# Decays counted from the middle of each two-chunk block, and a memory pool of their own for the joins, in a hybrid encoder layer

## The chip, the cores and the metric

The kernel runs on one core of one Trainium2 chip. The metric is the device time of one execution in microseconds (us). The engines are TensorE (PE, with its weight loads as PEld), VectorE (DVE), ScalarE (ACT), GpSimd (POOL) and SyncE (SP, which here only issues transfers). Each engine works through its own instructions in the order in which they stand in the program; an instruction that waits holds up everything behind it on its engine. SP and POOL issue loads and stores in their order too, and ACT issues some.

## The reference, cut to what matters

One layer: a SwiGLU feed-forward network, a mixer, and a second feed-forward network, on 1024 tokens of width 1024 in float32. The mixer projects its input once, computes attention on eight heads and a two-directional delta-rule scan (RWKV-7) on eight other heads, and projects both to the output. The change lies in the scan, whose step for one direction and head is

```python
def _rwkv7_step(state, inp):
    r, w, k, v, kk, kka = inp
    sa = jnp.einsum('dbhvk,dbhk->dbhv', state, kk)
    state = state * w[..., None, :] - sa[..., :, None] * kka[..., None, :] + v[..., :, None] * k[..., None, :]
    y = jnp.einsum('dbhvk,dbhk->dbhv', state, r)
    return state, y
...
    w_logit = w0 + jnp.einsum('bsdr,drc->bsdc', jnp.tanh(wd), w2)
    decay = jnp.exp(-jnp.exp(-jax.nn.softplus(-w_logit) - 0.5))
...
    h = h + 0.5 * _rmsnorm(f, ffn1_post_g[l])
    z = _rmsnorm(h, mix_pre_g[l]) @ w_in[l]
    y_att = _attention_group(z[..., :ATT_IN], cos, sin, attn_out_g[l])
    y_rwkv = _rwkv7_group(z[..., ATT_IN:], ...)
    mix = jnp.concatenate([y_att, y_rwkv], axis=-1) @ w_out[l]
    h = h + _rmsnorm(mix, mix_post_g[l])
```

The state is 64x64 per head and direction. Each step multiplies it by a decay, so that over several steps the product of decays, the exponential of a running sum of their logarithms, is what counts.

## The kernel before, in words

The sequence is cut into 16 chunks of 64 steps (C), and two chunks make one of 8 blocks (BLK = 2, TB = 128 steps). Both directions go side by side (d = 0 and 1), and eight heads are held as four pairs (pr) on the two halves of the partitions (par).

`low_rank` (lines 547 to 577) computes the logarithms of the decays for all steps, sums them up within each chunk with a scan along the row (line 576; `reset` starts the sum anew at each chunk) and stores the sums in HBM (`d_w`).

`prep` (lines 818 to 876) makes a block's operands, one direction after the other; a direction's part is called a prep half below. It loads the sums `cum` (the tile is named `th_w`) and the streams of keys, rates and receptances (`ka`, `kd`, `in`, the last from `d_rk`), and forms exp(cum) in `e` (line 840) and exp(-cum) in place (line 841). The column of `e` at a chunk's end, the decay over the whole chunk, is copied into `gc` (line 843), one column for each chunk. DVE multiplies kk and r by exp(cum) into `pr` (lines 845 and 846) and the keys and rates by exp(-cum) into `bk` (lines 849 and 851), ACT copies a piece of `bk` (line 850). PE then makes the scores `lp` (line 858), DVE masks them into `lm` (line 860), PE transposes `bk` into `bp` (line 866) and ACT copies that to `bt` (line 868). A piece of `lm` goes to HBM (`d_x`) and comes back as `X` in another layout.

`solve` (lines 878 to 898) inverts 64 triangular blocks of 32x32 on DVE in 31 pairs of short instructions on `ttmp` and `Ti` (lines 894 and 896) and a transpose (line 898).

`merge`, called the join below (lines 900 to 924), puts two inverses of 32 together to one of 64. Its matmuls are `pa` of lines 911, 916 and 922, its copies on ACT are `tt` of lines 912, 918 and 924 and `am` of line 919. The tile `am` lies in the pool `sc`, which the value streams' memory is given to once these are done.

`chain` (lines 938 to 994) is the sequential part. For each chunk PE computes `xu` from the chunk's scores and the state `sv` (line 963), ACT copies it to `xs` (line 966), PE multiplies by the joined inverse (`xu` again, line 974), ACT makes `uv` (line 976), and PE collects the new state in `st` and the outputs in `y` (both through the helper of line 959: `y<-pr,sv`, `st<-uv,bt`, `y<-lm,uv`). The old state is carried into `st` by a product with the identity (`st<-sv,ident`, all chunks but the first). DVE then makes the next state

```python
            if nx is not None:
                for par in range(2):
                    hs = half(par)
                    V.tensor_tensor(nx[hs, :, par], st[hs], gc[hs, :, :, i:i + 1].to_broadcast([64, 2, 4, 64]), op=OP.mult)
```

which is called the hand-over to the next chunk. The values come from HBM through loads of `uv` and `sv` that POOL issues (line 930).

Beside the chain lies other work: the prep halves of later blocks, their solves and joins, the attention half of the output projection (`project_attended`: `yat`, `yq`, `yah`, `yal`, `wol` and the matmuls `po`), and at the end the first finishing units (`yc`, `var`, `bonus`, `rstd`, `gate`) and the rest of the output projection (`pw`). Their order on each engine is set by a planner that gives each instruction a priority by its place in the code and a modelled cost, and puts it where it is expected to be ready; pools of memory hold a step back until their former users are done. No table written by hand sets it. The stages in time: the first feed-forward network to about 700 us, low-rank and value projections to 795, attention and the streams of the scan to 1180, the first preps from 1182, the joins and the chain from 1246 to 1549, finishing units and output projection to 1662, the second feed-forward network to the end.

## Time and profile before

| | us |
|---|---|
| median of 3 runs (2298.36 to 2302.42) | 2300.16 |
| the profiled execution's own time | 2300.81 |
| its span | 2299.0 |
| PE, DVE, ACT, POOL busy over the span | 2198.8, 1767.3, 1023.6, 537.0 |
| joins and chain, 1246.0 to 1548.5 | 302.5 |
| of this: before chunk 1's state is handed over (1292.8) | 46.8 |

Read the stage table by windows: for each stretch it gives an engine's busy time and number of instructions, the TensorE clock that was granted as a share of the full one, and the share of the transfer engines. The windows are cut where the second `sv` instruction of a hand-over to an even chunk ends. In a timeline row the first number is the start in us from the span's start and the second the time from the first start to the last end of the group; what stands in brackets is the idle time ahead of it and what ended it. PE's groups overlap by some tenths of a us, since matmuls are pipelined.

### The profile page before, as it was taken

The page shows a single profiled execution, that of the slowest core. Times are in us where ns is not written, and L with a number is a line of the kernel's source. Part 1 is how long each engine was busy: PE and PEld are TensorE (multiplying, and loading weights), DVE is VectorE, ACT ScalarE, POOL GpSimd, SP SyncE. Part 2 cuts the span into 40 slices and gives each one's busy share as a digit, 9 for nine tenths or more (in the row PEclk, how much of TensorE's full clock was granted, in tenths as well). Part 3 has the DMA queues.
Part 4 walks back from the last instruction along what each step waited for, and adds up shares of the span by engine and source line. Part 5 has one row for each costly group of instructions (what it writes and reads, how often), then busy time and mean ns, then how long its engine had stood idle before and what let it go on. Part 6 is the DMA issues. An engine that isn't in the chain of part 4 may idle for free. (4 is left out here: it accounts for less than half of the span.)

```text
span 2299.0 us, 41391 instructions
## 1 busy us (share of the span) xinstructions
PE 2198.8 (96%) x15556; PEld 1781.8 (77%) x15556; DVE 1767.3 (77%) x2893; ACT 1023.6 (45%) x1925; POOL 537.0 (23%) x673
## 2 busy tenths in 40 slices
PE   7999999999999998999998899999799999999998
PEld 5788888878877676777776777776678888888887
DVE  7999999865676254677679678747999999997566
ACT  5322323354567411666654644455442323335453
POOL 2354443410000011222221111122024444441000
PEclk9999999999999999999999799999899999999999
DMA  5354545486662513654467746357445454548665
GB/s 151 124 183 151 170 147 173 164 266 193 193 225 78 212 72 105 186 147 144 131 178 184 211 136 167 107 173 257 155 135 174 150 174 151 170 152 282 194 194 187
DMA packets 346700, 387.74 MB, mean 169 GB/s; under 512 B 73474, under 2 KB 249346, under 8 KB 346500
## 3 DMA queue, kind: packets, MB, share of 16 engines
q1 hardware_dynamic: 294928, 271.71, 39.2%
q0 software_dynamic: 31216, 100.73, 11.6%
q10 hardware_dynamic: 20356, 12.66, 1.8%
q8 instruction: 122, 2.00, 0.4%
q14 instruction: 78, 0.64, 0.1%
HBM read 258.06 MB, written 126.94 MB: 167 GB/s over the span
## 5 line engine op out<-in xcount | busy, mean ns | idle before, releaser
L81 PE MATMUL gu<-xh,wh 128*128 128x512 f32 x704 | 277.3, 394 | 4.6 <-ACT wh L186 4.5
L186 ACT ACTIVATE wh<-raw 128x512 fp32r<-128x512 f32 (+1 forms) x273 | 168.3, 627 | 252.3 <-PE gu L81 95.7
L81 PE MATMUL gu<-xl,wh 128*128 128x512 f32 x704 | 276.0, 392 | 0.0
L81 PE MATMUL gu<-xh,wl 128*128 128x512 f32 x704 | 275.9, 392 | 0.0
L187 DVE TENSOR_TENSOR wl<-raw,wh 128x512 fp32r<-128x512 f32 (+1 forms) x273 | 270.4, 994 | 3.7 <-ACT wh L186 3.0
L421 PE MATMUL pd<-gl,gwh 128*128 128x512 f32 x616 | 240.6, 391 | 2.6 <-DVE gl L187 2.6
L421 PE MATMUL pd<-gh,gwh 128*128 128x512 f32 x616 | 239.8, 390 | 0.6 <-DVE row L86 0.6
L421 PE MATMUL pd<-gh,gwl 128*128 128x512 f32 x616 | 240.1, 390 | 0.2 <-DVE gwl L187 0.2
L86 DVE TENSOR_TENSOR row<-gu,row 128x512 f32<-128x512 f32 x308 | 206.6, 683 | 25.8 <-PE gu L81 23.5
L187 DVE TENSOR_TENSOR gwl<-graw,gwh 128x512 fp32r<-128x512 f32 (+2 forms) x187 | 118.8, 643 | 124.0 <-ACT gwh L186 122.3
L116 POOL DMA_DIRECT2D d_hid<-row x154 | 84.7, 551 | 546.0 <-DVE row L114 524.2
L186 ACT ACTIVATE gwh<-graw 128x512 fp32r<-128x512 f32 (+2 forms) x187 | 103.1, 554 | 187.2 <-PE pd L421 151.3
L81 PEld LDWEIGHTS gu<-xh,wh 128*128 128x128 f32 x704 | 133.4, 190 | 33.6 <-ACT wh L186 5.6
L81 PEld LDWEIGHTS gu<-xh,wl 128*128 128x128 f32 x704 | 133.2, 189 | 27.7 <-DVE wl L187 0.2
L81 PEld LDWEIGHTS gu<-xl,wh 128*128 128x128 f32 x704 | 133.3, 189 | 27.4
L421 PEld LDWEIGHTS pd<-gl,gwh 128*128 128x128 f32 x616 | 115.7, 188 | 27.8 <-DVE gl L187 3.9
L421 PEld LDWEIGHTS pd<-gh,gwh 128*128 128x128 f32 x616 | 115.6, 188 | 25.5 <-DVE row L86 1.0
L421 PEld LDWEIGHTS pd<-gh,gwl 128*128 128x128 f32 x616 | 115.7, 188 | 24.1 <-DVE gwl L187 0.6
L187 DVE TENSOR_TENSOR gl<-raw,gh 128x512 fp32r<-128x512 f32 x160 | 114.7, 728 | 22.9 <-ACT gh L186 22.6
L94 ACT ACTIVATE row<-row 128x512 f32<-128x512 f32 x44 | 27.8, 633 | 212.0 <-DVE row L86 212.0
L145 POOL TENSOR_TENSOR ws<-ws 128x512 f32<-128x512 f32 x88 | 114.6, 1303 | 1.2
L186 ACT ACTIVATE gh<-raw 128x512 fp32r<-128x512 f32 x160 | 98.1, 622 | 35.5 <-DMA raw<-in_ffn_w_down_dram 22.8
(364 smaller groups left out, 5238.2 us busy)
## 6 DMA issues: line engine op xcount, KB each, us to landing
d_hid<-row POOLq DMA_DIRECT2D x154, 256.0 KB, 2.5
graw<-d_hid SPq DMA_DIRECT2D x132, 256.0 KB, 2.9
raw<-in_ffn_w_gate_dram SPq DMA_DIRECT2D x88, 256.0 KB, 3.1
raw<-in_ffn_w_up_dram SPq DMA_DIRECT2D x88, 256.0 KB, 3.6
ws<-in_ffn_w_down_dram SPq DMA_DIRECT2D x88, 256.0 KB, 4.1
d_ws<-ws POOLq DMA_DIRECT2D x88, 256.0 KB, 2.3
raw<-d_ws SPq DMA_DIRECT2D x88, 256.0 KB, 2.8
raw<-in_ffn_w_down_dram SPq DMA_DIRECT2D x66, 256.0 KB, 3.6
```

Source lines behind the costliest of these rows:

```text
L81: self.K.nc.tensor.matmul(ps, a[:, k, :], b[:, k, :], start=(k == 0 and i == 0), stop=(k == 3 and i == 2))
L86: add = lambda o, x: V.tensor_tensor(o, ps, x, op=OP.add)
L94: A.activation(y[:, 0], y[:, 0], AF.Silu)
L116: put = lambda n, y: G.dma_start(self.hid[n - 1, j // 2], y)
L145: G.tensor_tensor(o, a, b, op=OP.subtract)
L186: self.nc.scalar.activation(h, src, AF.Copy)
L187: (eng or self.nc.vector).tensor_tensor(l, src, h, op=OP.subtract)
L421: T.matmul(ps[x], a[:, ts], b, start=(m == 0 and k == 0), stop=(m == NM - 1 and k == 2))
```

## The change

Two things are changed. First, the sums of the first chunk of each block are shifted by the sum at that chunk's end (`mid`, kept in an unused piece of the tile `edge`), so that within a block all exponentials count from its middle. The state at the hand-over from an even to an odd chunk then needs no decay: `st` holds only the new products, and DVE adds the old state (`st` + `sv`). At the odd chunk's end the old state is still brought in by the identity product, and the decay of the second chunk and that of the next block's first are applied together: `gc` is the exponential of `cum`'s last column plus the next block's `mid`. Second, the join's tile `am` moves to a pool `joins` of its own, beside the two block pools.

In numbers: PE loses the four `st<-sv,ident` instructions of the seven even chunks after the first (28, which the trace records as 56). DVE gains eight copies of 128x8 and eight subtractions of 128x512 in `low_rank`; 16 `gc` copies become 14 additions of 128x4; the 30 state instructions are 2 copies, 14 products and 14 additions. ACT gains 16 exponentials of 128x4 and 7 of 128x8 (`gc`). POOL loses one memset. The transfers are the same in number. Since `gc` now reads `cum`, the exponential in place that follows it on ACT (line 846 of the changed kernel) comes after it.

```diff
@@ -574,6 +574,9 @@
                     V.tensor_tensor_scan(o, reset, o, 0.0, op0=OP.mult, op1=OP.add)
+                    first, mid = o.rearrange("p (n i t) -> p n i t", i=BLK, t=C)[:, :, 0], self.mid[:, d, pr]
+                    V.tensor_copy(mid, first[:, :, C - 1])
+                    V.tensor_tensor(first, first, mid[:, :, None].to_broadcast([128, NC_ // BLK, C]), op=OP.subtract)
                 self.nc.sync.dma_start(self.lr_d[nm][d][pr], o)
@@ -822,7 +825,7 @@
         lm = big.tile([128, 2, 2, BLK, 4, 128], F32, name="lm", tag="lm")
-        gc = big.tile([128, 2, 4, BLK], F32, name="gc", tag="gc")
+        gc = big.tile([128, 2, 4, BLK], F32, name="gc", tag="gc")[:, :, :, 0]
         blk = dict(lm=lm, pr=[], bt=[], gc=gc)
@@ -836,14 +839,15 @@
             e1 = self.e1
-            e4 = e1.rearrange("p (a i) t -> p a i t", i=BLK)
-            A.activation(e4[:, :, :, 1:C + 1], chunks(cum), AF.Exp)
+            if n + 1 < NC_ // BLK:
+                V.tensor_tensor(gc[:, d], cum[:, :, TB - 1], self.mid[:, d, :, n + 1], op=OP.add)
+            A.activation(e1[:, :, 0], self.mid[:, d, :, n], AF.Exp, scale=-1.0)
+            A.activation(e1[:, :, 1:], cum, AF.Exp)
             A.activation(flat(cum), flat(cum), AF.Exp, scale=-1.0)
             ei = chunks(cum)
-            V.tensor_copy(gc[:, d], e4[:, :, :, C])
             pt = big.tile([128, 4, BLK, 128], F32, name="pr", tag=f"pr{d}")
-            V.tensor_tensor(pt[:, :, :, 0:C], chunks(x["kk"]), e4[:, :, :, 0:C], op=OP.mult)
-            V.tensor_tensor(pt[:, :, :, C:], chunks(x["r"]), e4[:, :, :, 1:C + 1], op=OP.mult)
+            V.tensor_tensor(pt[:, :, :, 0:C], chunks(x["kk"]), chunks(e1[:, :, 0:TB]), op=OP.mult)
+            V.tensor_tensor(pt[:, :, :, C:], chunks(x["r"]), chunks(e1[:, :, 1:]), op=OP.mult)
             bk = p.tile([128, 4, BLK, 192], F32, name="bk", tag="bk", bufs=2)
@@ -868,6 +872,8 @@
                 blk[k].append(v)
+        if n + 1 < NC_ // BLK:
+            A.activation(gc, gc, AF.Exp)
         for par in range(2):
@@ -902,7 +908,7 @@
         NI, lm = 2 * BLK * 4, blk["lm"]
-        D, am = blk["inv"], p.tile([128, NI, 32], F32, name="am", tag="d11")
+        D, am = blk["inv"], p.tile([128, NI, 32], F32, name="am", tag="am")
         blk["tt"] = tt = self.tt[n % 2]
@@ -964,7 +970,7 @@
             A.copy(xs, xu)
-            if not first:
+            if i:
                 for d in range(2):
@@ -980,14 +986,19 @@
                 add(st[half(par), d, pr, :], bt[d][:, i, par, pr, :], uv[:, d, par, pr, :],
-                    first and d == 0 and pr == 0, True)
+                    not i and d == 0 and pr == 0, True)
             for d, pr, par in heads:
...
                     hs = half(par)
-                    V.tensor_tensor(nx[hs, :, par], st[hs], gc[hs, :, :, i:i + 1].to_broadcast([64, 2, 4, 64]), op=OP.mult)
+                    if i:
+                        V.tensor_tensor(nx[hs, :, par], st[hs], gc[hs, :, :, None].to_broadcast([64, 2, 4, 64]), op=OP.mult)
+                    elif first:
+                        V.tensor_copy(nx[hs, :, par], st[hs])
+                    else:
+                        V.tensor_tensor(nx[hs, :, par], st[hs], sv[hs, :, par], op=OP.add)
             for d in range(2):
@@ -1174,8 +1185,7 @@
         G, io = self.nc.gpsimd, self.io
-        self.e1 = p.tile([128, 4 * BLK, C + 1], F32, name="e1")
-        G.memset(self.e1[:, :, 0:1], 1.0)
+        self.e1 = p.tile([128, 4 * (TB + 2)], F32, name="e1").rearrange("p (a t) -> p a t", a=4)[:, :, :TB + 1]
         self.unit = p.tile([128, 2, 16], F32, name="unit")
@@ -1196,6 +1206,7 @@
             self.edge = self.pool(top, "edge", side="right").tile([128, 120], F32, name="edge")
+            self.mid = self.edge[:, 24:88].rearrange("p (d a n) -> p d a n", d=2, a=4)
             self.constants()
@@ -1271,7 +1282,7 @@
                 self.project_values(ring, psum, x, vw, range(5, NT))
-            s_mc, s_at, s_sc, s_ps = (ExitStack() for _ in range(4))
+            s_mc, s_at, s_sc, s_ps, s_mi = (ExitStack() for _ in range(5))
             self.mix_constants(self.pool(s_mc, "mixc", **R))
@@ -1290,6 +1301,7 @@
             R0, R1 = (self.pool(s_sr, f"blk{j}", 1, **R) for j in range(2))
+            mi = self.pool(s_mi, "joins", 1, **R)
             self.scan_constants(sp)
@@ -1317,18 +1329,19 @@
             rs_a = self.rstd(eo, self.ss_a.rearrange("p a b -> p (a b)"), NT * H, 1.0 / HD, EPS)
-            self.merge(0, blk[0], sc, pm)
+            self.merge(0, blk[0], mi, pm)
             upto(2)
...
                 if n + 1 < NB:
-                    self.merge(n + 1, blk[n + 1], sc, pm)
+                    self.merge(n + 1, blk[n + 1], mi, pm)
                 if n == NB - 1:
...
                     self.project_attended(eo, sc, pe, t, WA, rs_a)
+            s_mi.close()
             s_sr.close()
```

The order of the instructions moves with it, from the last projection of the streams to the end of the chain. Line numbers are those of the changed kernel in the rows of after. The counts here are instructions; the trace records two for each `lp`, `xu`, `pa`, `y` and `st`, and one for each `po`, `bp` and `yq`.

PE after the last matmul of the streams (`zr`), before: the first join's last two products (916, 922) stand behind the transposes of the values (`vt`) and among the scores of the third block.

```order
L523 MATMUL zr<-xh_5416,zl 128x512
L911 MATMUL pa<-ident,X 32x32 x64
L640 MATMUL vt<-ident,us 128x128 x8
L640 MATMUL vt<-ident,vrev 128x128 x4
L858 MATMUL lp<-pr,bk 128x128 x5
L640 MATMUL vt<-ident,vrev 128x128 x4
L858 MATMUL lp<-pr,bk 128x128 x11
L866 MATMUL bp<-ident,bk 128x64 x16
L916 MATMUL pa<-X,lm 32x32 x32
L858 MATMUL lp<-pr,bk 128x128 x6
L922 MATMUL pa<-tt_12073,am 32x32 x32
L858 MATMUL lp<-pr,bk 128x128 x10
```

And after: line 917 is the old 911, 922 the old 916, 928 the old 922.

```order
L523 MATMUL zr<-xh_5416,zl 128x512
L917 MATMUL pa<-ident,X 32x32 x64
L922 MATMUL pa<-X,lm 32x32 x32
L643 MATMUL vt<-ident,us 128x128 x8
L928 MATMUL pa<-tt_12097,am 32x32 x26
L643 MATMUL vt<-ident,vrev 128x128 x4
L928 MATMUL pa<-tt_12097,am 32x32 x6
L862 MATMUL lp<-pr,bk 128x128 x6
L643 MATMUL vt<-ident,vrev 128x128 x4
L862 MATMUL lp<-pr,bk 128x128 x10
L870 MATMUL bp<-ident,bk 128x64 x16
L862 MATMUL lp<-pr,bk 128x128 x16
```

The first join now stands ahead of most of the value transposes, and its copies on ACT likewise stand ahead of them; the join of the second block (the old 911) stands behind the chain's first `xu` where it stood ahead of it. On SP the load of `in` for the second half of the third block's prep stands ahead of the last four `d_vt` stores and no longer behind them.

DVE at the hand-over from chunk 7 to chunk 8, before: the `pr` products of the next prep half stand ahead of the hand-over, its scores are masked (860) right behind it.

```order
L990 TENSOR_TENSOR sv<-st,gc 64x2x256
L896 TENSOR_TENSOR Ti<-Ti,ttmp 128x21x6
L990 TENSOR_TENSOR sv<-st,gc 64x2x256
L894 TENSOR_TENSOR ttmp<-X,Ti 128x120
L843 COPY gc<-e_11074 128x8
L896 TENSOR_TENSOR Ti<-Ti,ttmp 128x20x6
L894 TENSOR_TENSOR ttmp<-X,Ti 128x133
L896 TENSOR_TENSOR Ti<-Ti,ttmp 128x19x7
L894 TENSOR_TENSOR ttmp<-X,Ti 128x126
L860 TENSOR_TENSOR lm<-lp,k_tri 128x512
L896 TENSOR_TENSOR Ti<-Ti,ttmp 128x18x7
L860 TENSOR_TENSOR lm<-lp,k_tri 128x512
```

And after: `gc` of both directions follows the hand-over (997 is the old 990), and the `pr` and `bk` products of the prep (849, 853, 855) come behind that.

```order
L997 TENSOR_TENSOR sv<-st,gc 64x2x256
L900 TENSOR_TENSOR ttmp<-X,Ti 128x96
L997 TENSOR_TENSOR sv<-st,gc 64x2x256
L902 TENSOR_TENSOR Ti<-Ti,ttmp 128x24x4
L843 TENSOR_TENSOR gc<-th_w,edge 128x4 x2
L900 TENSOR_TENSOR ttmp<-X,Ti 128x115
L1099 TENSOR_TENSOR yat<-yat,rs 128x512
L902 TENSOR_TENSOR Ti<-Ti,ttmp 128x23x5
L849 TENSOR_TENSOR pr<-in_14722,e_11093 128x8x64
L900 TENSOR_TENSOR ttmp<-X,Ti 128x110
L853 SCALAR_TENSOR_TENSOR bk<-ka,th_w 128x8x64
L902 TENSOR_TENSOR Ti<-Ti,ttmp 128x22x5
```

PE at the same place, before: the first prep half's scores stand between chunk 7's last product and chunk 8's `xu`, the second half's behind chunk 8's `xu`.

```order
L959 MATMUL y<-lm,uv 64x64 x16
L858 MATMUL lp<-pr,bk 128x128 x16
L866 MATMUL bp<-ident,bk 128x64 x8
L1091 MATMUL yq<-ident,yat 128x128 x2
L866 MATMUL bp<-ident,bk 128x64 x8
L1091 MATMUL yq<-ident,yat 128x128 x2
L963 MATMUL xu<-sv,lm 64x64 x16
L959 MATMUL st<-sv,ident 64x256 x4
L974 MATMUL xu<-xs,tt_12073 64x64 x16
L959 MATMUL y<-pr,sv 64x64 x3
L858 MATMUL lp<-pr,bk 128x128 x12
```

And after: chunk 8's `xu` comes first, and the scores of both halves follow it, ahead of the product with the joined inverse (980).

```order
L969 MATMUL xu<-sv,lm 64x64 x16
L965 MATMUL y<-pr,sv 64x64
L1091 MATMUL po<-woh,yah 128x512
L1091 MATMUL po<-wol,yah 128x512
L1091 MATMUL po<-woh,yal 128x512
L862 MATMUL lp<-pr,bk 128x128 x16
L870 MATMUL bp<-ident,bk 128x64 x8
L1091 MATMUL po<-woh,yah 128x512
L870 MATMUL bp<-ident,bk 128x64 x8
```

The second half's scores and transposes follow with eight more `po`, and then the product of line 980. The last prep, of block 7, stands whole at the end of chunk 9, ahead of chunk 10's `xu`. The `po` instructions are spread anew: counted from each chunk's first `xu`, over chunks 0 and 1, 2 and 3, 4 and 5, 6 and 7, 8 and 9, 10 and 11, and from 12 on, they are 12, 36, 36, 12, 24, 60, 12 before and 0, 48, 36, 24, 24, 48, 12 after. One finishing unit (`yc` to `gate`) more stands within the chain's last four chunks. From the end of the chain on, the order is the same, but for eight loads of `row` that SP issues earlier.

## The prediction

> **What bounds the kernel now.** I read the page first, then the stage table of the chain, the waits there, and the timelines of PE, DVE, ACT and SP at the two places that the order rows show. The page says that PE is the engine to watch:
>
> ```profile
> span 2299.0 us, 41391 instructions
> PE 2198.8 (96%) x15556; PEld 1781.8 (77%) x15556; DVE 1767.3 (77%) x2893; ACT 1023.6 (45%) x1925; POOL 537.0 (23%) x673
> ```
>
> The change leaves all but low-rank, the joins and the chain as they were, so the stage table decides. A row has the window and its length, then the busy time of PE, PEld, DVE, ACT and POOL, then the granted clock of PE, the share of the transfer engines and GB/s; the first two rows are the stage before chunk 0 and chunks 0 and 1, then come blocks 1 to 5 and chunk 12.
>
> ```profile
> 1246.00:1279.60 33.60, 23.38 (x497) 20.34 (x496) 24.48 (x65) 19.20 (x31) 8.04 (x14) 0.61 0.97 246
> 1279.60:1303.20 23.60, 21.59 (x455) 18.84 (x449) 14.02 (x31) 16.17 (x30) 3.69 (x7) 0.76 0.61 167
> 1303.20:1344.30 41.10, 39.69 (x744) 32.47 (x743) 34.23 (x106) 19.55 (x36) 5.81 (x12) 0.96 0.54 155
> 1344.30:1383.00 38.70, 35.70 (x724) 30.59 (x722) 27.82 (x82) 18.94 (x34) 5.82 (x12) 0.91 0.55 156
> 1383.00:1417.10 34.10, 31.84 (x712) 26.70 (x711) 27.79 (x85) 17.61 (x32) 5.32 (x12) 1.00 0.59 168
> 1417.10:1454.80 37.70, 35.05 (x718) 29.17 (x718) 29.56 (x88) 18.23 (x33) 5.53 (x12) 0.91 0.52 139
> 1454.80:1501.30 46.50, 42.51 (x745) 34.82 (x744) 34.67 (x107) 18.99 (x35) 5.21 (x9) 0.93 0.35 98
> 1501.30:1524.30 23.00, 20.21 (x448) 16.95 (x447) 6.83 (x23) 9.22 (x17) 8.00 (x11) 0.78 0.88 293
> ```
>
> In blocks 1 to 5 PE is busy for 91 to 97% and DVE for 72 to 83%: PE's work, its clock and its short waits make the time there. The part of a block lost to the clock, its length times what is missing to 1.00, is 1.6, 3.5, 0, 3.4 and 3.3 us, 11.8 in all. Ahead of chunk 0 PE stands for 10.2 of 33.6 us and runs at 0.61. Among the waits of the stage, 1246 to 1550, PE's own is that for the masked scores (in us, times, longest):
>
> ```profile
> PE lp L858 <- DVE lm L860: 4.5, 5, 1.1
> ```
>
> **The start of the chain.** The rows of several engines here, in order of time:
>
> ```profile
> 1246.12 1.29 PE L911 MATMUL pa<-ident,X 32*32 32x32 f32 x128
> 1251.12 1.09 PE L640 MATMUL vt<-ident,us 128*128 128x128 f32 x4 [3.72 <-DVE us L538]
> 1257.92 2.71 SPq L644 DMA_DIRECT2D d_vt<-vts  x4
> 1260.68 0.52 SPq L182 DMA_DIRECT2D in<-d_rk  x1
> 1265.56 0.57 ACT L912 COPY tt<-pa 128x512 f32<-128x512 f32 x1
> 1266.18 1.92 PE L916 MATMUL pa<-X,lm 32*32 32x32 f32 x64 [2.72 <-ACT tt L912]
> 1267.34 0.69 DVE L845 TENSOR_TENSOR pr<-in,e 128x512 f32<-128x512 f32 x1 [1.87 <-DMA in<-d_rk]
> 1270.92 1.92 PE L922 MATMUL pa<-tt,am 32*32 32x32 f32 x64
> 1277.76 1.93 PE L911 MATMUL pa<-ident,X 32*32 32x32 f32 x128
> 1279.61 1.18 PE L963 MATMUL xu<-sv,lm 64*64 64x64 f32 x19
> ```
>
> The first join is ready for its copy at 1247.4 (its `pa` of line 911 has run) and gets it 18 us later. In the new order the copy and the two products stand ahead of most value transposes, where PE stood for 3.72 us, so 1.92 + 1.92 = 3.84 us leave the path to the first `xu`. The load of `in` goes out ahead of four `d_vt` stores that take 2.71 us to issue, and that takes the wait of 1.87 out. Line 911 of the second join (1.93) moves from ahead of `xu` to behind it, where PE has other work to wait beside; I count nothing for it. The clock is the rest: the same 128 instructions take 1.29 us at 1246.12 and 1.93 at 1277.76, and with 3.72 us less of standing I take some of it back, 2.3 us. Together -8.0. What was late there, the prep of block 2, stays late, and DVE work that stood ahead of chunk 0 (two `wol`, `yat`, `yal`, two `bk`, about 6 x 0.69 = 4.2 us) comes later, into block 1, where DVE has 41.10 - 34.23 = 6.9 us free; I charge +1.0 of it. From -10 (the waits' whole 3.84 + 1.87 and a faster clock for the 13 us up to `xu`) to 0 (DVE, or the loads of the values that POOL issues behind the `d_vt` stores, hold the first `xu` back). The four stores go out 0.5 us later behind the load.
>
> **The identity products.** One chunk's four, in the chain of waits:
>
> ```profile
> 1542.54 1.01 PE st L959 x8
> ```
>
> Seven chunks lose it: 7 x 1.01 = 7.1. It stands where PE waits for ACT's copy `xs`, so not all is won: in the five even chunks 2 to 10 the scores and `po` now fill that gap, in 12 and 14 only `y` products do, which moves but removes nothing. I take -5.0, with 0 and -7.1 as ends. At the hand-overs the addition of `sv` costs DVE what the product did.
>
> **The prep behind the hand-over.** In the old order a prep half was ready before the hand-over and its scores filled PE right behind it. Rows at the hand-over to chunk 8 (1417.05):
>
> ```profile
> 1417.28 0.16 DVE L843 COPY gc<-e 128x8 f32<-128x8 f32 x1
> 1418.48 0.63 ACT L841 ACTIVATE th_w<-th_w 128x512 f32<-128x512 f32 x1
> 1419.45 1.04 PE L858 MATMUL lp<-pr,bk 64*128 64x128 f32 x7 [1.14 <-DVE lm L860]
> 1423.62 0.68 DVE L849 SCALAR_TENSOR_TENSOR bk<-ka,th_w 128x512 f32<-128x512 f32 x1
> 1427.28 0.62 ACT L850 COPY bk<-bk 64x512 f32<-64x512 f32 x1
> 1430.77 0.39 PE L1080 MATMUL po<-wol,yah 128*128 128x512 f32 x1
> 1431.00 0.40 PE L1080 MATMUL po<-woh,yal 128*128 128x512 f32 x1
> ...
> 1407.79 1.15 PE L963 MATMUL xu<-sv,lm 128*64 128x64 f32 x31
> ...
> L896 DVE TENSOR_TENSOR Ti<-Ti,ttmp 128x126 f32<-128x126 f32 (+22 forms) x206 | 52.4, 254 | 5.4
> ```
>
> In the new one, two `gc` (2 x 0.16), the exponential in place (0.63), `bk` (0.68) with `yat` (taken like `bk`), `pr` (0.69 as in line 845's row) and some solve steps between, and the copy of `bk` (0.62) follow the hand-over one after the other: 0.3 + 0.6 + 2.1 + 0.6, with three solve steps of 0.25 some 4.4 us. PE has for it the new chunk's `xu` (1.15 at full clock, as in block 3) and, of the 15 `po` around it, about eleven still to do at 0.23 from start to start (1430.77 to 1431.00), 3.7 together. So a wait of 0.7 us opens where one of 0.9 on average (4.5 in 5) closes, but two halves now follow each other, and DVE must bring 8 `lm`, 2 `pr` and 4 `bk` operations there, 14 x 0.68 = 9.5 us beside its solve steps, for about as much of PE's scores, transposes and `po`. I charge 0.8 us for each of five boundaries, +4.0; the ends are -4.5 (the waits of `lp` go and none comes) and +18 (first rival).
>
> **Moved `po`.** Block 5, the longest, gives away 12 of 60 instructions, 12 x 0.23 = 2.8 us; chunks 6 and 7, where PE had 34.10 - 31.84 = 2.3 us idle, take 12. Half is won: -1.4, between 0 and -2.8. The 12 that leave chunk 1 go to chunks 2 and 3; even.
>
> **The tail.** One finishing unit more lies among the chain's last chunks. A unit's own time on PE, from the chain of waits:
>
> ```profile
> 1548.48 1.06 PE yc L1014 x2
> 1551.60 0.79 PE var L1018 x8
> 1552.38 0.97 PE bonus L1025 x2
> 1554.30 0.88 PE gate L1039 x4
> ```
>
> That is 3.7 us from after 1548.5 to before it, where PE stood for 2.8 us of 23.0 at 1501.30. The steps behind the chain have waits of their own, so I take -2.5, between 0 and -3.7.
>
> **What I cost at nothing.** The 16 new operations in `low_rank`, 8 x (0.16 + 0.69) = 6.8 us of DVE, lie ahead of a stretch in which DVE has none to do (first row below; the second row, of 1500 to 1600, prices ACT's small operations):
>
> ```profile
> 756.50:794.60 38.10, 36.45 (x133) 24.00 (x131) 0.00 (x0) 14.54 (x22) 2.70 (x5) 1.00 0.45 173
> L1020 ACT ACTIVATE edge<-var,gneps 128x8 f32<-128x8 f32 x8 | 2.1, 268 | 5.7 <-PE var L1018 5.7
> ```
>
> PE does not wait for them there; without that cover they would cost their 6.8. ACT's 23 small exponentials cost 0.27 each, 6.2 us, on an engine that is busy for about half of each block; only where they stand in the line to `lp` do they count, and there they come ahead of it. Uncovered, +6.2. POOL's memset and DVE's `gc` copies go and come even.
>
> **The sum.** -8.0 + 1.0 - 5.0 + 4.0 - 1.4 - 2.5 = -11.9 against the profiled 2300.81, which is 1.81 over its span and 0.65 over the median: 2288.9 us.
>
> **Short waits and the clock.** At 1419.45 PE waited 1.14 us, and from 1421 to 1427 its clock stood at 0.50; at 1406.34 it waited 1.05 and block 3 stayed at 1.00:
>
> ```profile
> 1421.00:1427.00 6.00, 6.00 (x55) 4.34 (x55) 5.11 (x15) 3.26 (x6) 0.00 (x0) 0.50 0.43 115
> 1406.34 0.82 PE L916 MATMUL pa<-X,lm 32*32 32x32 f32 x39 [1.05 <-issue]
> ```
>
> So a wait of some 1.1 us goes with a half clock in one place and not in the other; 6 us at 0.50 cost 3 us. [...]
>
> **The rivals.** Slower: the chain gc, exponential, `bk`, copy opens waits of more than about 1 us ahead of `lp`, for both halves of each prep, and each is followed by 6 us at half clock. Two in each of five blocks cost 10 x 3 = 30 us where the blocks now lose 11.8, so +18 in place of +4: 2288.9 + 14 = 2303. It decides from a wait of about 1 us on, and 0.7 is my estimate; for it speaks the row at 1419.45, against it the one at 1406.34.
>
> No change: DVE sets the blocks. It is busy for 27.8 to 34.7 us in them and takes 4.2 us more over from before chunk 0; if the joins' gain only moves its work, -8 + 1 becomes -2 and the identity's -5 becomes -2: 2300.81 - 2 - 2 + 4 - 1.4 - 2.5 = 2297. For it speaks that DVE's solve of a block (31 x 2 steps of 0.25, 15.7 us) must be done before the next join; against it that PE, not DVE, is busy for 91 to 97%.
>
> The change does not do what it says: the first join stays late, because its tile `tt` is cleared by POOL at 1252 and later or its copies wait elsewhere. Then the -8 + 1 falls to -1 and the time is 2295. For it speaks POOL's row before, with the memset behind the last `d_v` store; against it that the memset now stands ahead of that store:
>
> ```profile
> 1252.02 1.86 POOL L1188 MEMSET tt<- 128x1024 f32 x2
> ```
>
> More gain: with `xu` ahead of the scores PE's short waits vanish, and the 11.8 us of clock come back: 2277.
>
> **How the numbers follow.** Forecast 0.45, around 2289 by 5 to either side; more gain 0.18; no change 0.12; late join 0.08; slower 0.17. About 0.2%, 4.6 us, is what a measurement can tell from no change here. Faster: 0.43 + 0.18 + 0.05 + 0.04 = 0.70; slower: 0.17, same the remaining 0.13. The range reaches from 2273, somewhat below the greater gain, to 2305, just above the slower rival, and leaves out what lies beyond two of these mishaps together.
>
> **What would show it.** The first `xu` of chunk 0 some 8 us earlier, near 1272, and the hand-over to chunk 1 near 1285 and not at 1292.8; no `st<-sv,ident` at the even chunks; waits of `lp` on `bk` or on ACT below 1 us; blocks 1 to 5 together about 197 us (198.1 before), the chain's end near 1539, and from there to the end 2.5 us less. Wrong would be a granted clock below 0.9 in most blocks, waits of PE above 1 us ahead of `lp`, or a first `xu` still at 1279.

## The result, and the profile after

The changed kernel takes 2311.43 us (median of five runs, 2309.86 to 2313.99) where the kernel before takes 2300.16. The ratio is 1.0053, 95% interval 1.0033 to 1.0072; one of the five executions of the kernel before, of 5375.53 us, is left out of it. The changed kernel is slower by half a per cent; 2289 and a range up to 2305 had been forecast. The profiled execution took 2309.86 us, so it stands for the runs. Its page, first and third line:

```profile
span 2308.1 us, 41327 instructions
...
PE 2201.0 (95%) x15500; PEld 1784.7 (77%) x15500; DVE 1772.0 (77%) x2907; ACT 1023.8 (44%) x1948; POOL 538.7 (23%) x672
```

PE has 56 instructions less and still 2 us more busy time. The stage table is cut as the one of before: the stage ahead of chunk 0, chunks 0 and 1, blocks 1 to 5, and then in one row the time from the hand-over to chunk 12 to the chain's end (columns: window and length, busy PE, PEld, DVE, ACT, POOL, granted clock, DMA share, GB/s).

```profile
1245.40:1270.50 25.10, 18.89 (x354) 16.55 (x353) 20.69 (x59) 17.01 (x30) 7.18 (x11) 0.66 0.88 238
1270.50:1299.60 29.10, 21.69 (x577) 19.55 (x576) 13.72 (x32) 17.11 (x31) 5.40 (x11) 0.77 0.66 178
1299.60:1342.70 43.10, 40.42 (x734) 33.40 (x734) 36.06 (x107) 21.08 (x40) 5.01 (x11) 0.96 0.52 153
1342.70:1388.30 45.60, 39.22 (x711) 32.84 (x710) 27.56 (x80) 19.23 (x37) 5.62 (x12) 0.81 0.48 136
1388.30:1427.60 39.30, 35.28 (x711) 29.89 (x710) 27.20 (x82) 18.50 (x36) 5.94 (x12) 0.91 0.52 147
1427.60:1470.80 43.20, 36.05 (x641) 30.77 (x639) 31.50 (x89) 17.49 (x33) 5.97 (x11) 0.77 0.57 154
1470.80:1515.20 44.40, 42.27 (x808) 35.02 (x807) 38.05 (x123) 19.88 (x37) 5.24 (x9) 0.96 0.30 85
1515.20:1563.70 48.50, 44.85 (x966) 36.27 (x964) 17.14 (x32) 26.37 (x50) 16.43 (x22) 0.89 0.84 287
```

Blocks 1 to 5 take 43.1 + 45.6 + 39.3 + 43.2 + 44.4 = 215.6 us where they took 198.1: 17.5 more. That is more than the 9.1 us by which the spans differ. The rest went the right way: the hand-over to chunk 2 comes at 1299.6 (1303.2 before), and from the chain's end to the end of the span pass 744.3 us (750.6). Blocks 2 to 4 carry the loss, and blocks 2 and 4 have a clock of 0.81 and 0.77 (both 0.91 before). Among PE's waits in joins and chain, 1245 to 1564 (in us, times, longest), these five lead:

```profile
PE pa L917 <- issue: 8.2, 2, 4.4
PE lp L862 <- DVE bk L855: 6.4, 3, 3.9
PE pa L922 <- issue: 6.0, 4, 2.3
PE pa L928 <- issue: 2.6, 2, 1.6
PE lp L862 <- DVE ttmp L900: 2.6, 1, 2.6
```

Two kinds of wait have grown: that of the scores `lp` for the prep's `bk` (0.4 us before), and a wait put down to "issue", in which PE waits for nothing that the profile knows (16.8 us in these rows, 6.4 before; in blocks 1 to 5 alone 9.7 and 4.5). The row for `ttmp` lies ahead of block 1.

**The prep at a hand-over.** Rows of DVE, ACT and PE at the hand-over to chunk 4, in order of time:

```profile
1341.98 0.69 DVE L997 TENSOR_TENSOR sv<-st,gc 64x512 f32<-64x512 f32 x1
1342.91 0.24 DVE L843 TENSOR_TENSOR gc<-th_w,edge 128x4 f32<-128x4 f32 x2
1343.39 1.15 ACT L846 ACTIVATE th_w<-th_w 128x512 f32<-128x512 f32 x2 [0.76 <-DVE Ti L902]
1346.52 0.69 DVE L849 TENSOR_TENSOR pr<-in,e 128x512 f32<-128x512 f32 x1 [1.85 <-DMA in<-d_rk]
1347.33 0.68 DVE L853 SCALAR_TENSOR_TENSOR bk<-ka,th_w 128x512 f32<-128x512 f32 x1
1348.05 0.62 ACT L854 COPY bk<-bk 64x512 f32<-64x512 f32 x1 [2.92 <-DVE bk L853]
1348.88 3.78 PE L862 MATMUL lp<-pr,bk 64*128 64x128 f32 x24 [3.93 <-DVE bk L855]
```

And the 6 us from the start of these scores, and the next 6, as windows (the clock is the third number from the end):

```profile
1348.90:1354.90 6.00, 6.00 (x30) 5.03 (x31) 4.93 (x13) 1.83 (x4) 0.00 (x0) 0.50 0.85 248
1354.90:1360.90 6.00, 6.00 (x33) 4.39 (x33) 3.40 (x10) 1.17 (x2) 0.00 (x0) 0.50 0.35 100
```

`gc` starts within 0.3 us of the end of the hand-over, and `pr`, `bk`, the copy and `lp` follow one after the other. `gc` lies in the memory of the block, which goes round among three blocks, so it can't be written before the hand-over three blocks back has read its own. It now also reads `cum`, and so the exponential in place, and everything behind that, waits with it. PE stands for 3.93 us and then runs for 12 us at half clock. At the hand-over to chunk 8, which ends at 1427.56, the wait is 2.23 us and the clock 0.50 for the next 6 us; two operations of DVE wait there for their loads:

```profile
1429.25 0.69 DVE L1099 TENSOR_TENSOR yat<-yat,rs 128x512 f32<-128x512 f32 x1 [1.06 <-DMA yat<-d_ya]
1431.64 0.69 DVE L849 TENSOR_TENSOR pr<-in,e 128x512 f32<-128x512 f32 x1 [1.51 <-DMA in<-d_rk]
1433.96 4.28 PE L862 MATMUL lp<-pr,bk 64*128 64x128 f32 x29 [2.23 <-DVE bk L855]
```

Not all of the clock lost in the blocks follows the prep. In block 4 PE also stood in a join, for an issue wait, and ran the next 6 us at half clock:

```profile
1463.71 0.54 PE L917 MATMUL pa<-ident,X 32*32 32x32 f32 x21 [3.78 <-issue]
1463.80:1470.00 6.20, 6.20 (x151) 5.84 (x152) 2.36 (x7) 3.66 (x7) 1.19 (x2) 0.50 0.19 51
```

**Chunk 0.** PE from the first `xu` on, and DVE's state for chunk 1:

```profile
1270.45 0.32 PE L969 MATMUL xu<-sv,lm 64*64 64x64 f32 x2
1273.74 1.17 PE L917 MATMUL pa<-ident,X 32*32 32x32 f32 x114
1279.29 0.43 PE L917 MATMUL pa<-ident,X 32*32 32x32 f32 x14 [4.37 <-issue]
1284.78 1.92 PE L928 MATMUL pa<-tt,am 32*32 32x32 f32 x64 [1.12 <-ACT am L925]
...
1288.64 1.41 DVE L999 COPY sv<-st 64x512 f32<-64x512 f32 x2 [13.13 <-PE st L965]
```

The first `xu` stands 9.2 us earlier than before (1279.61), and the hand-over ends at 1290.1, only 2.7 earlier (1292.8): the second join lies between the two, with a standing of 4.37 us within the instructions of one line.

### The profile page after: what moved, and what is told of

It reads as the page before. It is cut to its first block, busy times and chain, and to the rows that moved or that the text cites. A ratio compares the mean times of both kernels' runs of the same rounds, so it can differ in the third digit from the quotient of the medians.

```text
span 2308.1 us, 41327 instructions
## 1 busy us (share of the span) xinstructions
PE 2201.0 (95%) x15500; PEld 1784.7 (77%) x15500; DVE 1772.0 (77%) x2907; ACT 1023.8 (44%) x1948; POOL 538.7 (23%) x672
## 4 chain that ended last, share of the span: by engine, by line
PE 40%; DVE 5%; DMA 3%; issue 2%; ACT 2%; SPq 0%; POOL 0%; DVEq 0%; ACTq 0%; POOLq 0%
PE gu L81 18%; PE pd L421 9%; PE zr L523 1%; PE po L1091 1%; PE lp L862 1%; PE pw L1091 1%; PE st L965 1%; DVE Ti L902 1%; DVE ttmp L900 1%; DMA in<-d_rk 1%; PE y L965 1%; PE xu L980 1%; PE xu L969 1%; PE bp L870 1%; DVE lm L864 1%
```

## The experiments

The theory after the traces: `gc`, held by an older hand-over, costs the blocks (held prep). Its rivals: the new arithmetic as such (additions for the identity product), the joins' pool, and the issue waits, which I took for a late supply of instructions. All ratios are to the kernel before, run beside each on the same chip.

**The two parts apart.** First the decays from the middle without the joins' pool (from the changed kernel):

```diff
-        D, am = blk["inv"], p.tile([128, NI, 32], F32, name="am", tag="am")
+        D, am = blk["inv"], p.tile([128, NI, 32], F32, name="am", tag="d11")
...
-            mi = self.pool(s_mi, "joins", 1, **R)
...
-            self.merge(0, blk[0], mi, pm)
+            self.merge(0, blk[0], sc, pm)
...
-                    self.merge(n + 1, blk[n + 1], mi, pm)
+                    self.merge(n + 1, blk[n + 1], sc, pm)
```

> The decays counted from the middle, without the pool for the joins (the first join late again, its tile in the scan's memory). Theory 1, held prep: `gc` now reads `cum`, its tile is free only after the hand-over of an earlier block, and so the exponential in place, `bk` and the scores wait behind each hand-over. By it this kernel keeps the PE waits ahead of `lp` of 2 to 4 us behind several hand-overs and is slow: 2310 to 2316, since it also loses the 3 us of the earlier hand-over to chunk 1. Theory 2, instruction supply: PE stands with nothing to wait for at every 256th instruction where small matmuls of the joins lie close together, because the join was moved. By it the standing named issue goes back from 16.8 us towards the 6.2 of before, and the kernel is at 2300 to 2304.

Then the joins' pool alone, the opposite edit made to the kernel before:

> The pool for the joins alone, decays counted as before. Theory 1, held prep: no `gc` reads `cum`, the scores stand right behind the hand-overs as before, and only the earlier start of the chain is left: 2294 to 2298, with the hand-over to chunk 1 near 1289. Theory 2, instruction supply: the join's small matmuls stand close to the chain's, issue waits of 12 us or more in all, and the kernel is at 2304 to 2310.

Measured: 1.0080 (1.0062 to 1.0098) for the decays alone, with blocks 1 to 5 at 212.1 us and 12.6 us of `lp` waits; 1.0046 (1.0025 to 1.0067) for the pool alone, with a first `xu` at 1272.8, 6.8 us earlier, and a hand-over to chunk 2 at 1304.9, later than before. Neither part is a gain alone, and the losses don't add up to that of both. The decays bring the loss in the blocks; why the pool alone costs isn't shown by this run.

**The identity product alone.** The even chunks of the kernel before leave out `st<-sv,ident`, and with it the carry of the old state there:

```diff
-            if not first:
+            if i:
...
-                    first and d == 0 and pr == 0, True)
+                    not i and d == 0 and pr == 0, True)
```

> The kernel before without the product with the identity at the even chunks, so the old state is not carried over there (this part of the computation is left out); nothing else is changed. It prices the 28 products alone: my prediction's term says -5 us, 2295, between 2293 (all 7.1 us) and 2300 (none). Theory 1 and theory 2 say the same here; if it gains nothing, the product was free and the whole gain from the middle is nothing but moved work.

Measured: 1.0009 (0.9997 to 1.0022). To leave out the products of seven chunks is worth nothing that can be told.

**`gc` freed.** The changed kernel with `gc` in a tile of its own that rotates over four blocks:

```diff
-        gc = big.tile([128, 2, 4, BLK], F32, name="gc", tag="gc")[:, :, :, 0]
+        gc = p.tile([128, 2, 4], F32, name="gc", tag="gc", bufs=4)
```

> The changed kernel with one edit: `gc` lies in a tile of its own with four buffers in the prep's pool and no longer in the block's, so that it can be written before the hand-over that still reads an older one. Theory 1, held prep: the prep half's scores stand right behind the hand-over again, PE's waits ahead of `lp` fall to about 1 us each, and the time falls by 10 to 16 us to 2295 to 2301. Theory 2, instruction supply: the joins stay where they are, so the time stays within 3 us of 2311.

Measured: 1.0065 (1.0050 to 1.0080), yet blocks 1 to 5 at 198.0. What the blocks won was lost behind: 14.1 us from the hand-over to chunk 15 to the chain's end (8.4 in the changed kernel) and 758.4 us from there (744.3). PE waited there for a finishing unit:

```profile
1545.02 2.07 PE L1025 MATMUL yc<-f_y,k_cen 128*128 128x512 f32 x2 [4.21 <-POOL f_y L1024]
```

The same edit on the decays alone, and the same edit with the finishing units' loads of `f_y` issued by SP and not by POOL, to see whether POOL's queue was the reason:

```diff
-            (self.nc.gpsimd if nm[0] == "y" else self.nc.sync).dma_start(z[nm], src[ps2, :, sl].rearrange("a p t -> p a t"))
+            self.nc.sync.dma_start(z[nm], src[ps2, :, sl].rearrange("a p t -> p a t"))
```

> Decays from the middle alone (no joins pool), with gc in a rotating tile of four of its own, so that it waits for no hand-over. Theory (held prep): the wait of gc for the hand-over three blocks back is what cost the blocks; blocks 1 to 5 come to 195 to 201 us in place of 212.1 with the same change without the free gc, the PE waits of lp to below 9 us from 12.6, and the time to 2299 to 2304 from 2317. Rival (additions on DVE in place of the identity product, or the shifted exponentials as such): blocks stay at 208 or more, time at 2312 or more. A loss behind the chain, as in the kernel with joins pool and free gc, may add up to 10 us to the time, not to the blocks.

> The changed kernel with gc in a rotating tile of four, and with the finishing units' loads of f_y issued by SP in place of POOL. Theory (POOL's queue): the 5.7 us lost between chunk 15 and the chain's end and most of the 14 us lost behind the chain, against the changed kernel, come from f_y loads that POOL issues behind the loads of the last chunks' values; by that the time falls from 2313 to 2301 to 2306, and PE's wait of 4 us ahead of the first yc goes. Rival (the transfers themselves, or the order of the finishing units): time stays at 2310 to 2315 with the wait ahead of yc as it was. Blocks 1 to 5 stay near 198 us by either.

Measured: decays alone with `gc` freed 1.0057 (1.0036 to 1.0078) with blocks at 196.0 us in place of 212.1, and 759.8 behind the chain: the blocks as forecast, the time not. With SP's loads 1.0040 (1.0023 to 1.0057): PE still waits 3.4 us for `f_y`, and the time behind the chain stays at 758.5. POOL's queue was not the main reason. SP's queue shows what was: the first load of the finishing units, `g2w`, waits there for a hand-over (waits of SP in 1490 to 1550, kernel with `gc` freed; then the row of SP's timeline),

```profile
SPq L182 <- DVE sv L997: 13.3, 1, 13.3
```

```profile
1533.78 0.33 SPq L182 DMA_DIRECT2D g2w<-in_rwkv_g_dram  x1
```

My edit had put `gc` into the prep's pool, and it held that memory, which the finishing units take over, until its last reader. So `gc` went into a piece of the tile `edge` that nothing uses:

```diff
-        gc = big.tile([128, 2, 4, BLK], F32, name="gc", tag="gc")[:, :, :, 0]
+        gc = self.edge[:, 88 + n % 4 * 8:96 + n % 4 * 8].rearrange("p (d a) -> p d a", d=2)
```

> The changed kernel with gc in an unused piece of the tile edge, four blocks' worth, so that it neither waits for a hand-over nor lies in the scan's pool. Theory: (1) blocks 1 to 5 stay near 198 us as with gc in a rotating tile of the scan's pool; (2) the loss behind the chain there came from gc itself: the finishing units' memory overlaps that pool, so their first load (g2w) waited for the last hand-overs that read gc (13.3 us on SP's queue). Here that load goes out before 1520, the time behind the chain falls from 758 to 745 to 752, and the kernel comes to 2299 to 2305 from 2313. Rival (the finishing units are late for another reason): behind the chain 756 or more, time 2308 or more.

> Decays from the middle alone (no joins pool), with gc in the unused piece of edge. Theory as for the kernel with both parts: blocks 1 to 5 near 196 to 200 us, behind the chain 745 to 752 in place of 759.8 with gc in the scan's pool, time 2293 to 2300 from 2308.5, at or below the kernel before. Rival: behind the chain stays at 756 or more and the time at 2305 or more.

> The kernel with gc in edge once more, beside the one with the late join, on the same chip. As in its first runs: ratio to before 0.998 to 1.001, median 2293 to 2299; if the second run differs from that by more, the size of what gc costs is known to no better than that.

Measured: 0.9998 (0.9982 to 1.0013) with both parts, and 0.9988 (0.9973 to 1.0003) when it ran again beside another kernel; 1.0019 (1.0004 to 1.0034) with the decays alone. In the first, `g2w` goes out at 1515.66, 748.0 us pass behind the chain, and blocks 1 to 5 take 198.8:

```profile
1303.20:1344.80 41.60, 40.92 (x756) 34.77 (x754) 38.33 (x119) 20.20 (x40) 6.70 (x13) 0.96 0.61 174
1344.80:1383.30 38.50, 33.10 (x699) 28.53 (x699) 24.89 (x72) 20.33 (x39) 4.82 (x10) 0.91 0.51 140
1383.30:1422.00 38.70, 35.95 (x712) 30.65 (x710) 29.18 (x88) 19.09 (x36) 5.45 (x12) 0.87 0.53 153
1422.00:1459.90 37.90, 34.47 (x713) 29.58 (x713) 28.62 (x85) 18.68 (x35) 5.58 (x12) 0.91 0.52 141
1459.90:1502.00 42.10, 39.70 (x734) 32.76 (x731) 34.55 (x104) 17.48 (x32) 4.68 (x9) 1.00 0.37 104
```

PE at the hand-over to chunk 4 (1344.8) in this kernel:

```profile
1342.76 2.05 PE L862 MATMUL lp<-pr,bk 64*128 64x128 f32 x24
```

The scores run ahead of the hand-over again, 2.05 us for what took 3.78; the next scores still wait 2.65 us for the masks `lm`, at 1348.10. As the kernel stands, moving this one small tile takes the whole loss away, and the change is then level with the kernel before, no faster. In the profiled executions blocks 1 to 5 take 203.3 to 224.7 us in the six in which `gc` is held and 192.2 to 198.8 in the seven in which it isn't (those further down among them, but for the one with the late join). The move of `gc` also moves the issue waits, though: in blocks 1 to 5 they come to 9.7 us in the changed kernel and to 3.8 here. What the held prep costs by itself these two runs don't tell.

**The issue waits.** PE resumed from each of the eight at a place a whole number of 256 PE instructions from the others (number 193 of 256 each time, counted in the trace with weight loads and semaphore steps), as if a block of 256 began there. If that is the cause, instructions added anywhere ahead shift the waits through the code. First 32 small matmuls (128 PE instructions, half a block) and then 64 (a whole block, with 65 and 64 in place of 33 and 32) ahead of the first norm:

```diff
-            self.nc.tensor.matmul(q, one, r[:1], start=True, stop=True)
+            for k in range(33 - 32 * c): self.nc.tensor.matmul(q[:, :32] if k < 32 - 32 * c else q, one, r[:1, :32] if k < 32 - 32 * c else r[:1], start=True, stop=True)
```

> The changed kernel, with 32 small matmuls added far ahead of the chain (at the constants, before the first feed-forward network's end), which with their weight loads and nothing else shift PE's later instructions by 64 to 128 positions; the order of the joins and the chain is unchanged. Theory (supply of PE's instructions): the waits that the trace puts down to issue happen where a new block of 256 PE instructions begins, so they move in the code by the shift: the wait of 4.37 us inside the second join's line 917 at 1279.29 is no longer at its 100th or so product, and new waits of 1 to 4 us stand at other rows. Rival (something at that place in the code, a semaphore or a transfer, holds PE): the wait of about 4 us stays at the same product of line 917. The time is within 6 us of the changed kernel's 2311 by either; the first theory lets it differ by that much for the sum of the issue waits (16.8 us) is drawn anew, the second has it within 2 us plus about 2 us for the added matmuls.

> The same with 64 small matmuls, twice the shift, which is meant to be one whole block of 256 PE instructions. Theory (supply of instructions): the waits put down to issue come back to the same products as in the changed kernel, 4 us inside the second join's line 917 among them. Rival (place in the code): the same, as in the run with half the shift; only that run and this one together tell them apart. A third theory, that any added instruction disturbs the planner's order and so the waits, has both runs differ from the changed kernel. Time within 3 us of the changed kernel's, plus about 3 us for the matmuls.

Measured: 1.0078 (1.0058 to 1.0098) and 1.0167 (1.0131 to 1.0203); the added matmuls stand in the path at the start, and the last `zr` of the streams ends 11.7 and 22.2 us later, 0.51% and 0.97%. The waits of joins and chain put down to issue, all of them, with half a block and then with a whole one:

```profile
PE xu L969 <- issue: 2.3, 2, 1.2
PE y L965 <- issue: 1.6, 2, 1.4
PE pa L917 <- issue: 1.4, 1, 1.4
PE pa L922 <- issue: 1.2, 1, 1.2
PE pa L928 <- issue: 0.2, 1, 0.2
```

```profile
PE pa L922 <- issue: 7.2, 4, 2.3
PE pa L917 <- issue: 7.0, 2, 3.9
PE pa L928 <- issue: 2.3, 2, 1.2
PE xu L980 <- issue: 0.6, 1, 0.6
```

Half a block moves most of them to other products and brings them to 6.7 us; a whole block brings back the same lines with 17.1. So the waits belong to the blocks of 256, not to the place in the code. What they cost was to be measured with 32 matmuls of 32x32 at the very start, where PE waits for its first loads (2.22 us in the changed kernel) and the order of everything else stays; in the changed kernel, in the kernel before, in the kernel with `gc` in `edge`, and with the changed kernel itself once more beside the last:

```diff
-        t = p.tile([128, D], F32, name="s_" + name)
+        t = p.tile([128, D], F32, name="s_" + name); z = psum.tile([128, 512], F32, name="pt", tag="t", bufs=2)[:32, :32]; [self.nc.tensor.matmul(z, one[:, :32], one[:, :32], start=True, stop=True) for k in range(32)]
```

> The changed kernel with 32 matmuls of 32x32 (128 PE instructions, half a block of 256) at the very start, where PE waits for the first loads; every other instruction stands in the same order on every engine. Theory (supply of PE's instructions): as in the run with half a block ahead of the first norm, the waits put down to issue in the joins and the chain fall from 16.8 to about 7 us and blocks 1 to 5 from 215.7 to about 203, and since these matmuls delay nothing at the start, the time falls by 6 to 11 us, to 2300 to 2305. Rival (the position of the instructions does not matter, the earlier run differed because its start was delayed): time within 2 us of 2311, issue waits 15 us or more.

> The same 32 matmuls at the start of the kernel before. Theory (supply of PE's instructions): the waits put down to issue in the joins and the chain, 6.4 us, are drawn anew at other rows; the kernel before may win or lose some us by it, within 2293 to 2308, and if it loses, the drawn position explains part of the difference between the two kernels. Rival (the kernel before is not sensitive to it): within 2 us of 2299, with the waits at the same rows as before.

> The changed kernel once more, beside the runs that follow. Theory: 0.5% slower than before as in its first runs (ratio 1.0033 to 1.0072), median 2308 to 2314. Rival (its first five runs were close together by chance, and it scatters like the one with 32 matmuls at the start): median 2302 to 2307, so that the position of the instructions would be worth nothing that can be told.

> The changed kernel with gc in the unused piece of edge, and 32 matmuls of 32x32 at the start, so that PE's later instructions stand half a block of 256 further on. Theory (held prep and position add up): the wait put down to issue of 4 us in the second join goes, chunk 1's state is handed over 3 to 5 us sooner after the last matmul of the streams (46.3 us now), the time falls by 3 to 7 us from 2296, to 2289 to 2293, ratio to before 0.996 to 0.998. Rival (position is worth nothing by itself, or other rows get stalls of the same sum): 2294 to 2300, ratio 0.998 to 1.001.

Measured: changed kernel with the shift 1.0032 (1.0014 to 1.0050), without it 1.0050 (1.0030 to 1.0070); kernel before with the shift 1.0031 (1.0011 to 1.0052); `gc` in `edge` with the shift 1.0009 (0.9985 to 1.0034), without it 0.9998 and 0.9988. In the profiled executions the issue waits fell from 16.8 to 6.7, rose from 6.4 to 10.1, and fell from 14.8 to 5.4 (the profiled execution of the first took 2315 us, at the upper end of its runs, 2297 to 2316, so its blocks, 214.2 us, say little). So the shift moves the waits each time, and the ratios by 0.1 to 0.3% in either direction. For the changed kernel some 4 us of the 6 to 11 that I expected came, by the ratios, and the intervals overlap; for the kernel with `gc` in `edge` 9 us less of such waits brought no gain; and in the kernel before the last `zr` of the profiled execution ends 4.6 us later with the shift, so not all of its loss need come from waits in the joins. How much of the 0.5% these waits are stays open: 0.2% by the ratios, between nothing and 0.4% by their intervals.

One thing more stands in these numbers. With the same shift in both, the changed kernel (1.0032) and the kernel before (1.0031) are level, and `gc` in `edge` is worth 0.2% there (1.0032 to 1.0009, with overlapping intervals), not the 0.5 to 0.6% of the kernels without the shift. So the half per cent belongs to these two kernels as they stand. The held prep lengthens the blocks in every run; its cost apart from where the issue waits fall lies somewhere between nothing and 0.6%.

**The second join out of chunk 0.** With `gc` in `edge`, the join of the second block is called behind the first block's chain:

```diff
-                if n + 1 < NB:
+                if 0 < n < NB - 1:
...
                 self.chain(n, blk.pop(n), sc, pc)
+                if not n:
+                    self.merge(1, blk[1], mi, pm)
```

> The changed kernel with gc in the unused piece of edge, and the join of the second block called behind the chain of the first block and not ahead of it, so that its products stand behind chunk 0's. Theory (the start's gain was given back to the second join, whose products and copies stand in chunk 0's path): from the first xu to the hand-over to chunk 1 takes 13 to 16 us in place of 21.9, that hand-over comes at 1285 to 1289 and the one to chunk 2 at 1299 to 1302 in place of 1303.2; the time falls by 1 to 4 us from 2296, to 2292 to 2295. Rival (the join is only put off, and its 6 us are paid before chunk 2): the hand-over to chunk 2 stays at 1303 or later and the time at 2295 to 2299.

Measured: 1.0041 (1.0026 to 1.0057), slower than its control. The hand-over to chunk 1 did come at 1286.9 and that to chunk 2 at 1295.2, 8.0 us earlier than in the first run of the kernel with `gc` in `edge` and 6.9 earlier than in the control, its second run; but block 1 then took 51.2 us (40.7 in the control):

```profile
1295.20:1346.40 51.20, 45.54 (x817) 38.64 (x817) 42.14 (x134) 25.88 (x48) 6.26 (x13) 0.87 0.56 153
```

Against the row of `gc` in `edge` above it has 817 - 756 = 61 more PE instructions, 4.6 us more busy time and a clock of 0.87, not 0.96. An earlier start of the chain only moved work beside it into block 1, and the hand-over to chunk 4 came at 1346.4, not at 1344.8 (1342.8 in the control). The issue waits moved too: in blocks 1 to 5 they are 9.1 us, 3.0 in the control. Which of these makes up the 0.4% at the end is not settled.

A double buffer for `in`, aimed at the wait of `pr` for its load, wasn't tried. Of all these kernels, none beats the kernel before by more than can be measured.

## Why the prediction was wrong

**The prep behind the hand-over, +4.0: the mechanism was named, its size was wrong.** The step said that a wait of 0.7 us opens at each of five hand-overs. Two above 1 us opened, of 3.93 us at chunk 4 and 2.23 at chunk 8, and the blocks went up by 17.5 us. With `gc` in `edge` they take 198.8, so the term measured 215.6 - 198.8 = 16.8 us in the place of 4.0 as these kernels stand, the issue waits that moved along included. The sum in the step failed at three places. Its line from the hand-over to `lp` was 4.4 us; it took 6.2 at chunk 4 and 6.4 at chunk 8, since `pr`, priced at 0.69, waits another 1.85 and 1.51 us for its load, `yat` at chunk 8 another 1.06, and the second `bk` (line 855) was left out. Its cover was 3.7 us, with eleven `po`; at chunk 8 they are there, and PE had work for 4.2 us, but at chunk 4 no `po` stands between the hand-over and `lp`, and `xu` and `y` gave 2.3. And it priced a wait without its clock, which was my estimate: 3.93 us of standing were followed by 12 us at 0.50, which cost as much again and more, and 2.23 us by 6 us at 0.50.

**No term for the issue waits.** They were 6.4 us in the kernel before, and the working shows one of them, at 1406.34; what a new order does to them was put at nothing. They came to 16.8, 9.7 of them in blocks 1 to 5. An edit that holds no prep back can cost nearly as much as this change: the joins' pool alone is at 1.0046, the shift alone at 1.0031.

**The rival's chance.** The slower rival had this place and this mechanism with 0.17. That its +18 is close to the 17.5 measured is partly luck: it counted ten waits with 6 us of half clock each, and two came, longer ones, with issue waits beside them. Its own time, 2303, was too low because the gains it kept did not come either.

**The gains that did not come.** Without the +4.0, the other terms promise 15.9 us. With `gc` in `edge` the change is worth 0.5 and 2.8 us (0.9998 and 0.9988 of 2300.16). So more than half of the 22.5 us by which the forecast missed lies in these terms.

**The start of the chain, -8.0 + 1.0.** The first `xu` came 9.2 us earlier, as the step said. The gain ended there: that line 911 of the second join moves behind `xu` was counted at nothing, but it brings its whole join with it, since the copies on ACT and the two later products follow. From the first `xu` to the hand-over took 19.6 us in place of 13.2, 4.37 of them the issue wait within the join. That wait alone is not the reason: with `gc` in `edge` chunk 0 has one of 4.67 us and the hand-over comes 46.3 us after the last `zr`; with the shift the wait is gone, and the hand-over comes after 46.9. At the hand-over to chunk 2, 3.6 us of the 9.2 were left. With the join moved out, 8 us were won there and lost within block 1: the rival "no change", in which the work beside the chain sets the blocks, is nearer to this than the forecast; that DVE is what sets them, as that rival says, isn't shown (PE is busy for 45.5 of the 51.2 us of block 1 there, DVE for 42.1).

**The identity products, -5.0.** The run without them is at 1.0009: worth between 0.7 us of gain and 5 us of loss, by its interval. The end of the range was right, the middle was not. That the work to fill PE's wait for `xs` is not always ready would explain it; no run shows it.

**The tail, -2.5.** From the hand-over to chunk 12 to the end of the span pass 792.8 us, before 797.7: -4.9, beyond the term's end. That the finishing unit made this gain isn't shown: no run prices it alone, and the two profiled executions of the kernel with `gc` in `edge` differ by as much there (796.6 and 801.8). It was not free: the row 1515.20 is 48.5 us for 47.2.

**Moved `po`, -1.4.** Block 5 went from 46.5 to 44.4; what the other blocks lost by it can't be told from the held prep.

**At nothing.** The 16 operations in `low_rank` cost nothing that can be told: the last `zr` ended at 1245.5, 0.7 us earlier than before. That the first join stays late (0.08) did not happen, and no clock came back (0.18). Of the signs given for a wrong forecast, one was seen, waits above 1 us ahead of `lp`; the clock was below 0.9 in two blocks and not in most.

## What to carry to other kernels

A tile that goes round among the blocks carries its last reader's time into its next writer: when a change gives a small result a new reader or an earlier place, ask where its memory comes from, and follow everything that reads the same source behind it. Count as cover of a wait only what the engine's own order puts ahead of the waiting instruction at that place; here it was eleven `po` at one hand-over and none at another. A gain ahead of a pipeline is a gain only if the first block behind it has room; here the first `xu` won 9 us and the end nothing. And before half a per cent is put down to a cause, measure what an edit that only shifts the instructions does: here 0.1 to 0.3% by the ratios.

## What was not expected of the hardware

PE's instructions seem to arrive in blocks, and where PE runs many short ones the supply shows. Over the whole changed kernel, a queue of the kind "instruction" moved

```profile
q8 instruction: 122, 2.00, 0.4%
```

that is 122 pieces, 2.00 MB. The trace holds 31,303 PE instructions, weight loads and semaphore steps among them, 257 for each piece, so I take this queue for PE's. Of the 122 places in the trace that are number 193 of 256, PE stood at eight, for 0.9 to 4.4 us, all of them in the joins and the chain, where the 256 instructions ahead of the place had passed in 1.6 to 4.1 us; and the standings moved with the number of instructions ahead, from 16.8 us to 6.7 with half a block and to 17.1, at the same lines, with a whole one. At the other 114 places PE has no gap above 0.15 us. Busy transfer engines are not needed for a standing: their share is 0.99 in the one of 4.4 us before 1279.29, and 0.12 in that of 2.3 us before 1414.67. At 1279.29 a piece had been moving from 1276.66 on, for 1.15 us, when PE already stood, and PE resumed 1.48 us after its end (1.25 to 1.52 us after a piece's end in all eight). If that piece held the instructions PE stood for, it was asked for late or held up by other transfers; which, the trace doesn't tell.

The second is the length of the half clock. After 3.93 us of standing it lasted for 12 us, after 2.23 us for 6 at 0.50 and 6 more at 0.66, so with what the clock took (6 us and 3 + 2) these waits cost 9.9 and 7.3 us, two and a half and three times their length.
